# Four held chunks in the output projections, next-stage windows by token tile, and tails as tasks

## The chip, the cores and the metric

The kernel runs on one core of one Trainium2 chip. The metric is device microseconds of one execution, the median of several runs. Engines: TensorE (PE, matmuls; PEld its weight loads), VectorE (DVE), ScalarE (ACT), GpSimd (POOL), and SyncE (SP), whose queue issues the DMAs.

## What is computed

Two transformer-like layers on 256 tokens of width 1024, in float32. The parts that the change touches are the output projections, the residual with its norm behind them, and the first products of the next stage:

```python
# layer 1, end of the mixer
mix = (g_ssd * y_ssd + g_sc * y_sc) @ w_o
x = x + gt1 * rmsnorm(mix, mix_post_g)
h = rmsnorm(x, ffn_pre_g) * (1.0 + sc2) + sh2
u = causal_dwconv(h @ w_up, ffn_conv_w, ffn_conv_b)
u_gate, u_val = jnp.split(u, 2, axis=-1)
f = (jax.nn.silu(u_gate) * u_val) @ w_down
x = x + gt2 * rmsnorm(f, ffn_post_g)
# layer 2
h = rms_norm(x, attn_norm) * (1.0 + scale_a) + shift_a
... = jnp.split(h @ w_in, IN_OFFSETS, axis=-1)          # nc, ns, nw, q, ...
x = x + gate_a * (o @ w_o)                              # no norm on the product
h = rms_norm(x, ffn_norm) * (1.0 + scale_f) + shift_f   # then a second conv FFN, gated by gate_f
```

The modulation rows and columns (gt1, sc2, ...) are products of silu(c) with 1024x1024 blocks of `ada_w` ("ada" below).

## The kernel before

**Weights.** All weights stream from HBM in order of the list `keys`: chunks of 128x2048, each in two halves of 128x1024 (512 KB). `dma_next` loads a half into one of six `raw` tiles. `cast_next` (line 527) splits it: ACT writes `hi` (rounded to fp32r), DVE writes `lo` = raw - hi, into one of five `hlp` slots (HALVES = 5); `caster` does so whenever fewer than `limit[0]` halves are ahead. Each product is three matmuls (hi x hi, lo x hi, hi x lo). A key "ada" isn't cast: `ada_mul` multiplies the half by silu(c) on DVE with a running sum.

**Two product forms.** `chunk_a` (643): weights stationary, 256 token columns moving, 48 matmuls of 128x256 for a chunk of 2x128 features. `b_mm`, `window` and `out_proj`: 128 tokens stationary, 512 weight columns moving, output by token tile t = 0, 1.

**Order.** The instruction streams are written out by a planner (`_Order`): the main code issues PE's work; tasks (generators) issue the work of DVE, ACT and the transposes when their planned time is reached, by rank. Each engine then runs its stream in order.

**Output projections.** `out_proj` (679) runs three times: "wo" (4 chunks, end of the mixer), "dn" (11 chunks, end of the first FFN), "wo2" (4 chunks, end of attention), and "dn2" closes the kernel. All chunks but the last two run for both token tiles; the last two are held in SBUF, all of tile 0's products run first, then tile 1's 24 matmuls of 128x512. `tail_of(t)` follows each.

**Tails.** `tail` (1471) makes the next normalized activations (`h2`, `h3`, `h4`, as hi and lo) of a token tile from the projection in PSUM: square and row sum (`sq`), times the gate row (`mul`), `norm_sum` (POOL raises to -1/2), residual update (`upd`), square of x (`sqx`), `norm_sum`, a diagonal matrix of the norm (`diag`), transposing matmuls x.T @ diag (`turn`), scale and shift (`evA` on ACT, `evV` on DVE), `hi`, `lo`. For "wo2" there is no first norm. The order of these steps, and where weight casts stand among them (`cast:`), is written out by hand in the strings TAILS (line 245); casting is otherwise off (`limit[0] = 0`).

**Filler.** The rows gt2 and gf don't come through `keys`. `adp` (1027) loads their eight halves into `adp` tiles, `adp_add` sums 6 or 7 of them on DVE, and `adp_fill` puts the rest on PE as float32 matmuls of 128x512 inside the tails of "wo" and "wo2" (`fill:`). The other rows are spread over the partitions by `row_sum` (1044) with 8 small matmuls.

**Behind the tails.** In `ffn` (1647) the first two up chunks run in parts ("0a 0b 1a ..."), each on both tiles at once, so they start when both tiles are turned. Behind "dn", `window_split` (1754) runs "nc" for tile 0, lets the tail go on, then for tile 1; "ns" and "nw" follow as windows. `w1` needs the blocks that `nc_task` makes from nc. `wo2_ready` (2402) waits for the tasks `os_task(g, t)`, which make the two halves of the attention output: wo2's chunks 0 and 1 need group 0, chunks 2 and 3 need group 1.

Of the kernel before, what the change touches and what calls it, by code (L numbers as in the profile page):

```python
# [26 lines left out]


ON_PE = ("gt2", "gf")


def _plan():

    plan = []
# [44 lines left out]
    for i in range(22):  # L79
        plan.append((("up", i), 2048, a_pair("w_up", 128 * i, 2816 + 128 * i)))  # L80
# [23 lines left out]
    for i in range(22):  # L104
        plan.append((("up2", i), 2048, a_pair("w_up_2", 128 * i, 2816 + 128 * i)))
# [5 lines left out]
    for nm, (w, s) in {**ADA_ROW, **ADA_COL}.items():  # L111
        for j in range(4):
            plan.append((("ada", nm, j), 2048, b_cols(w, 2 * j, 2, 1024 * s, 1024) if nm in ON_PE else f_rows(w, 1024 * s + 256 * j)))
# [94 lines left out]
def _consts():  # L208
# [33 lines left out]
UPORDER = ("0a 0b 1a 0l 1b 1l", "0a 0b 1a 1b 0l 1l")  # L242
LAST_C = "gt1"
ND = {"gt2": 6, "gf": 7}
TAILS = {
# [170 lines left out]
def _body(ctx: ExitStack, tc: tile.TileContext, wst, pf_d, rows_d, cst_d, xT_d, x_d, w2_d, out_d):  # L416
# [86 lines left out]
    st = {"dma": 0, "cast": 0, "half": 0, "ahead": 0}  # L503
# [23 lines left out]
    def cast_next():  # L527
# [5 lines left out]
        if keys[i][0] == "ada":  # L533
            ada_mul(keys[i][1], 2 * keys[i][2] + hf, r)
        else:
            h = hlp.tile([128, 1024], F32R, name="hi")
            l = hlp.tile([128, 1024], F32R, name="lo")
# [30 lines left out]
    def drop(i, hf):  # L568
        parts.pop((i, hf))
        st["ahead"] -= 1  # L570
        free_at[0] = O.t["pe"]
# [107 lines left out]
    def out_proj(name, nch, x, ready, tail_of, done=lambda c: None):  # L679
# [12 lines left out]
        for c in range(nch - 2):  # L692
            ready(c, 0)
            ready(c, 1)

# [4 lines left out]
            done(c)  # L700
        held = []
        for c in (nch - 2, nch - 1):
# [3 lines left out]
        for t in range(2):  # L706
            for c in (nch - 2, nch - 1):
                ready(c, t)
            for j in range(2):
                for w, c, hf in held:  # L710
# [30 lines left out]
    for w, g in SSD_ORDER:  # L741
        keys += [("scc", g), ("sch", g), ("scb", g)] if w == "sc" else [(w, g, 0), (w, g, 1)]
    so = lambda p: [("so", p, 0), ("so", p, 1)]
# [4 lines left out]
    keys += [("wo", k) for k in range(4)] + [("up", i) for i in range(22)] + [("dn", k) for k in range(11)]  # L748
# [6 lines left out]
    keys += [("up2", i) for i in range(22)] + [("dn2", k) for k in range(11)]  # L755
# [15 lines left out]
    assert sorted(map(str, keys)) == sorted(str(k) for k, _, _ in PLAN if k[0] != "ada0" and k[1] not in ON_PE)  # L771

# [116 lines left out]
    for t in range(8):  # L889
        w = W(t)  # L890

        def half(hf_):
# [7 lines left out]
            st["ahead"] -= 1  # L900

# [16 lines left out]
    limit = [HALVES]  # L918
# [49 lines left out]
    adp_w, adp_sum, adp_ps = {}, {}, {}  # L968

    def adp_load(nm, spared):  # L970

        for k in range(8):
            yield from room(big=1 + spared)
            r = big("adp")
            O.keep("big")
            o, n = CH["ada", nm, k // 2]
            nc.sync.dma_start(r, bass.AP(tensor=wst.tensor, offset=wst.offset + o + 1024 * (k % 2), ap=[[n, 128], [1, 1024]]))
            adp_w[nm].append((r, O.dma(512, O.cur.now)))
            O.cur.now = max(O.cur.now, O.t["dma"] - 1500.0)
# [1476 lines left out]
```

## Time and profile before

| | |
|---|---|
| median of 3 runs | 1071.05 us (1067.59 to 1071.38) |
| the profiled execution | 1072.64 us, of it the span from first to last instruction 1070.7 us |
| PE busy | 1036.2 us (97%), 7183 matmuls |
| DVE busy | 849.8 us (79%) |
| ACT busy | 628.4 us (59%) |
| mean granted clock of PE | 0.982 |

Matmuls are pipelined, so a matmul's cost is the distance from one start to the next, not its duration. PE without a gap isn't PE at its best either: small or needless matmuls count as busy.

### The profile page before, as it was taken

To read this page: it belongs to the slowest core of one execution; us is meant where nothing else is said; L and a number is where in the kernel's file an instruction comes from. 1 tells how busy PE (TensorE), PEld (TensorE's weight loads), DVE (VectorE), ACT (ScalarE), POOL (GpSimd) and SP (SyncE) were. 2 spreads that over 40 slices of the span, in tenths; PEclk is the share of its full clock that TensorE was granted. 3 is DMA by queue.
4 is the path that set the end of the run, shared out by engine and by line. 5 is a ranking of instruction groups with operands and counts; after the bars stand their busy time and mean duration, and the time that the engine had idled before them with its cause. 6 is when DMAs were issued, how large, how long until landed. Compare 5 with 4: busy or idle time off the path is not lost.

```text
span 1070.7 us, 18920 instructions
## 1 busy us (share of the span) xinstructions
PE 1036.2 (97%) x7183; PEld 957.1 (89%) x7183; DVE 849.8 (79%) x1566; ACT 628.4 (59%) x1230; POOL 45.7 (4%) x66
## 2 busy tenths in 40 slices
PE   7999999999999999999999889998999789999998
PEld 7999999899999979999987779877998679999986
DVE  5878978977987768998886888896889687878843
ACT  3457569378654366656554466768675346666531
POOL 2000000000000000000000010221100000000000
PEclk8999999999999999999999989998999989999999
DMA  9855577767868947676686588854256725555551
GB/s 356 310 197 170 176 244 242 238 208 242 284 211 305 328 171 227 223 262 222 225 302 201 188 304 281 291 204 139 77 159 231 281 91 195 180 181 183 188 185 40
DMA packets 66187, 234.03 MB, mean 219 GB/s; under 512 B 7568, under 2 KB 8624, under 8 KB 65584
## 3 DMA queue, kind: packets, MB, share of 16 engines
q1 hardware_dynamic: 66096, 232.82, 64.4%
q8 instruction: 56, 0.92, 0.3%
q14 instruction: 35, 0.29, 0.1%
HBM read 230.67 MB, written 2.13 MB: 217 GB/s over the span
## 4 chain that ended last, share of the span: by engine, by line
PE 52%; DVE 5%; ACT 3%; DMA 2%; issue 1%; POOL 0%; ACTq 0%; DVEq 0%; POOLq 0%
PE ps L410 52%; DVE lo L410 2%; DMA raw<-in_wst_dram 1%; ACT hi L410 1%; DMA adp<-in_wst_dram 1%; ACT S L410 1%; DVE S L410 1%; ACT jk L410 0%; DVE raw L410 0%; DVE jk L410 0%; DVE ropet L410 0%; DVE qo L410 0%; DVE Sm L410 0%; DVE tmp L410 0%; ACT tmp L410 0%
## 5 line engine op out<-in xcount | busy, mean ns | idle before, releaser
L410 DVE TENSOR_TENSOR lo<-raw,hi 128x1024 fp32r<-128x1024 f32 (+3 forms) x326 | 388.2, 1197 | 149.0 <-ACT hi L410 147.9
L410 ACT CAST hi<-raw 128x1024 fp32r<-128x1024 f32 (+3 forms) x326 | 332.9, 1031 | 216.2 <-PE ps L410 170.5
L410 PE MATMUL ps<-hh,hi 128*128 128x256 f32 (+1 forms) x520 | 152.8, 294 | 4.1 <-ACT hh L410 4.1
L410 PE MATMUL ps<-hl,hi 128*128 128x256 f32 (+1 forms) x520 | 148.8, 286 | 0.5 <-DVE hl L410 0.4
L410 PE MATMUL ps<-hh,lo 128*128 128x256 f32 (+1 forms) x520 | 148.6, 286 | 0.0
L410 PEld LDWEIGHTS ps<-hh,hi 128*128 128x128 f32 (+1 forms) x520 | 100.4, 193 | 5.9 <-ACT hh L410 4.5
L410 PE MATMUL ps<-h4h,hi 128*128 128x256 f32 x352 | 100.9, 289 | 2.8 <-ACT h4h L410 2.8
L410 PEld LDWEIGHTS ps<-hl,hi 128*128 128x128 f32 (+1 forms) x520 | 100.4, 193 | 2.3 <-issue 1.2
L410 PE MATMUL ps<-h4h,lo 128*128 128x256 f32 x352 | 100.7, 288 | 0.0
L410 PEld LDWEIGHTS ps<-hh,lo 128*128 128x128 f32 (+1 forms) x520 | 100.4, 193 | 0.1
L410 PE MATMUL ps<-h2h,hi 128*128 128x256 f32 x352 | 98.4, 283 | 0.0
L410 PE MATMUL ps<-h2h,lo 128*128 128x256 f32 x352 | 98.3, 283 | 0.0
L410 PE MATMUL ps<-h2l,hi 128*128 128x256 f32 x352 | 94.7, 283 | 0.0
L410 PE MATMUL ps<-h4l,hi 128*128 128x256 f32 x352 | 94.5, 283 | 0.0
L410 DVE CUSTOM_DVE_ANT_0 raw<-raw,crow 128x1024 f32<-128x1024 f32 x64 | 76.9, 1219 | 0.0
L410 DVE SCALAR_TENSOR_TENSOR fc<-ps,pf,fc 128x254 f32<-128x254 f32 (+1 forms) x176 | 72.4, 474 | 0.0
L410 PEld LDWEIGHTS ps<-h4h,hi 128*128 128x128 f32 x352 | 69.6, 198 | 3.0 <-ACT h4h L410 3.0
L410 PEld LDWEIGHTS ps<-h4h,lo 128*128 128x128 f32 x352 | 69.5, 197 | 0.0
L410 PEld LDWEIGHTS ps<-h2h,hi 128*128 128x128 f32 x352 | 67.6, 192 | 0.8 <-ACT h2h L410 0.8
L410 PEld LDWEIGHTS ps<-h2h,lo 128*128 128x128 f32 x352 | 67.6, 192 | 0.0
L410 PEld LDWEIGHTS ps<-h2l,hi 128*128 128x128 f32 x352 | 65.4, 192 | 0.0
L410 PEld LDWEIGHTS ps<-h4l,hi 128*128 128x128 f32 x352 | 65.4, 192 | 0.0
(394 smaller groups left out, 2363.6 us busy)
## 6 DMA issues: line engine op xcount, KB each, us to landing
raw<-in_wst_dram SPq DMA_DIRECT2D x364, 512.0 KB, 4.9
adp<-in_wst_dram SPq DMA_DIRECT2D x16, 512.0 KB, 7.2
ada0a<-in_wst_dram SPq DMA_DIRECT2D x8, 512.0 KB, 8.0
ada0b<-in_wst_dram SPq DMA_DIRECT2D x8, 512.0 KB, 8.7
E<-scr SPq DMA_DIRECT2D x4, 1024.0 KB, 6.8
raw<-in_wst_dram SPq DMA_DIRECT2D x8, 400.0 KB, 7.5
raw<-in_wst_dram SPq DMA_DIRECT2D x8, 384.0 KB, 7.3
brow<-in_rows_dram SPq DMA_DIRECT2D x4, 512.0 KB, 7.9
```

The source lines that it names most:

```text
L410: return f(*a, **k)
```

## The change

- `out_proj` holds four chunks instead of two ("wo", "dn", "wo2"; "dn2" stays at two): tile 0 runs all held products first, then tile 1 runs 48 matmuls of 128x512. A chunk of the first two held is dropped during tile 1's pass.
- Weight halves beyond five may be cast into pairs of `big` tiles (22 of 128x1024 in all, shared with the activations) while `more[0]` is set and `spared` tiles are left over.
- The tail of each tile is a task (`tail_task`, rank -0.8) whose steps go out as they come due. x is scaled by the norm on ACT and DVE and then transposed (`transpose`, one pass) instead of turned by a diagonal matrix. The strings TAILS, the filler and `adp` are gone. Casting is no longer switched off.
- The next stage begins with two products of 512 columns (`windows`): tile 0 of both, then tile 1 of both. Behind "dn" these are nc and ns. In the FFNs they are the first four up chunks in the 512-column form ("upb"); their outputs are copied by ACT and transposed on PE (`copy_task`, `turn_task`) to the layout that `up_task` wants.
- The rows gt2 and gf come through `keys` like the others (`ada_mul`, then `row_sum` with its 16 small matmuls for two halves), at new places: gt2 behind up 4, sha behind up 11, sca behind up 18, shf behind dn 3 (it was behind ns 0), gf behind up2 10. The activation row is switched from c to c2 behind gt2 (it was behind gt1).
- The tiles of attention that `wo2_ready` released are released by a task.

```diff
+    def up_plan(key, w):
+        for p in range(2):
+            cols = np.concatenate([np.arange(256) + o + 256 * p for o in (0, 2816)])
+            for h in range(2):
+                plan.append(((key + "b", p, h), 2048, b_list(w, 4 * h, 4, cols)))
+        for i in range(4, 22):
+            plan.append(((key, i), 2048, a_pair(w, 128 * i, 2816 + 128 * i)))
...
+SPARED = {"gt1": 6, "gt2": 3, "ga": 3}
+HOLD_GA = 4
+LAST_C = "gt2"
...
+            inner = st["hl"] < HALVES
+            if inner:
+                h, l = hlp.tile([128, 1024], F32R, name="hi"), hlp.tile([128, 1024], F32R, name="lo")
+            else:
+                h, l = big("whi", F32R), big("wlo", F32R)
...
-            yield lambda: st["ahead"] < limit[0] and st["cast"] in raws
+            yield lambda: st["cast"] in raws and (st["hl"] < HALVES or more[0] is not None and O.used["big"] + 2 + more[0] <= CAP["big"])
...
-        for c in range(nch - 2):
+        for c in range(nch - hold):
             ready(c, 0)
             ready(c, 1)
+            if c == nch - hold - 2:
+                more[0] = spared
...
+        more[0] = spared
         held = []
-        for c in (nch - 2, nch - 1):
+        for c in range(nch - hold, nch):
...
         for t in range(2):
+            for w, c, hf in held[:-4]:
+                if not hf:
+                    ready(c, t)
+                if not t:
+                    arrive(w, hf)
+                half(t, w, c, hf)
+                if t:
+                    drop(w.i, hf)
...
-    mix_in("sha", ("up", 8), 2)
-    mix_in("sca", ("up", 20), 4)
+    mix_in("gt2", ("up", 4), 2)
+    mix_in("sha", ("up", 11), 2)
+    mix_in("sca", ("up", 18), 2)
+    mix_in("shf", ("dn", 3), 1)
     mix_in("ga", ("bg", 5), 1)
     mix_in("scf", ("q1", 1), 1)
-    mix_in("shf", ("ns", 0), 2)
+    mix_in("gf", ("up2", 10), 2)
...
+        def tail_task(t, ps):
...
+            r = norm_sum(ss)
+            yield
+            par(lambda: AC.activation(tmp[:, :512], x[:, :512], AF.Identity, scale=r),
+                lambda: VE.tensor_scalar(tmp[:, 512:], x[:, 512:], r, None, op0=OP.mult))
...
+            for f in range(8):
+                transpose(tp[f // 4][:, 128 * (f % 4):128 * (f % 4) + 128], tmp[:, 128 * f:128 * f + 128])
...
+    def windows(names, x, ks, done):
...
+        for t in range(2):
+            O.until(lambda: len(ks) > t and ks[t].done)
+            for n in range(2):
+                ps = bank()
+                for q, (w, hf) in enumerate(held[n]):
+                    arrive(w, hf)
+                    for k in range(2):
+                        kk = 2 * q + k
+                        O.pump()
+                        x.come(kk, 0, (t,))
+                        xh, xl = x.hi(kk, 128 * t, 128), x.lo(kk, 128 * t, 128)
+                        c = hf * 1024 + k * 512
+                        PE.matmul(ps, xh, w.hi(c, 512), start=kk == 0, stop=False)
+                        PE.matmul(ps, xh, w.lo(c, 512), start=False, stop=False)
+                        x.come(kk, 1, (t,))
+                        PE.matmul(ps, xl, w.hi(c, 512), start=False, stop=kk == 7)
...
+        windows([(up + "b", p) for p in range(2)], hh, k_hh, done)
...
-        for i in range(2, 22):
-            ks.append(O.spawn(up_task(i, chunk_a((up, i), hh), w, b, first_is_gate, f)))
+        for i in range(4, 22):
+            ks[i] = O.spawn(up_task(i, chunk_a((up, i), hh), w, b_, first_is_gate, f))
...
-    k_nc = O.spawn(nc_task(window_split("nc", k_h)))
...
+    windows([("nc",), ("ns",)], h, k_h, pw_done)
...
-    adp("gf", 2)
-    out_proj("wo2", 4, osum, wo2_ready, of)
+    out_proj("wo2", 4, osum, wo2_ready, of, hold=HOLD_GA, spared=SPARED["ga"])
```

## Rows read from the trace of the kernel before

**Rows 1.** The page, part 1: busy us, share of span, instructions.

```profile
PE 1036.2 (97%) x7183; PEld 957.1 (89%) x7183; DVE 849.8 (79%) x1566; ACT 628.4 (59%) x1230; POOL 45.7 (4%) x66
```

**Rows 2.** PE's waits: what it waited for, us in total, times, longest.

```profile
PE ps L410 <- DVE Sm L410: 4.4, 3, 3.7
...
PE ps L410 <- DVE ko L410: 4.0, 1, 4.0
```

**Rows 3.** Stretches: length; busy us of PE, PEld, DVE, ACT, POOL; granted clock; DMA.

```profile
398.50:460.00 61.50, 61.50 (x512) 61.50 (x513) 53.39 (x86) 39.01 (x59) 0.00 (x0) 1.00 0.70 224
460.00:526.00 66.00, 66.00 (x550) 65.87 (x548) 58.79 (x103) 39.95 (x66) 0.00 (x0) 1.00 0.73 242
526.00:585.30 59.30, 59.30 (x263) 48.81 (x261) 43.25 (x71) 28.20 (x42) 1.08 (x2) 1.00 0.74 250
...
876.60:882.80 6.20, 6.16 (x29) 6.16 (x30) 4.71 (x6) 3.36 (x4) 0.00 (x0) 0.50 0.39 131
```

**Rows 4.** Timeline of PE, wo's end to up's start: start, us, operation [idle before].

```profile
387.52 0.39 PE L410 MATMUL ps<-hi,mixl 128*128 128x512 f32 x1
...
388.20 0.39 PE L410 MATMUL ps<-hi,mixl 128*128 128x512 f32 x1
389.16 2.05 PE L410 MATMUL ps<-btok,xr 128*128 128x128 f32 x16 [0.58 <-DVE btok L410]
391.05 3.60 PE L410 MATMUL ps<-adp,cb 128*128 128x512 f32 x8
394.70 2.05 PE L410 MATMUL ps<-btok,xr 128*128 128x128 f32 x16
...
398.48 0.39 PE L410 MATMUL ps<-h2h,hi 128*128 128x256 f32 x1
398.70 0.28 PE L410 MATMUL ps<-h2h,lo 128*128 128x256 f32 x1
...
398.94 0.28 PE L410 MATMUL ps<-h2h,lo 128*128 128x256 f32 x1
```

**Rows 5.** Timeline of PE, dn's end to the second tile of nc.

```profile
585.29 2.05 PE L410 MATMUL ps<-btok,xr 128*128 128x128 f32 x16
...
590.20 0.50 PE L410 MATMUL ps<-hi,h3h 128*128 128x512 f32 x1 [2.85 <-ACT h3h L410]
...
599.26 0.50 PE L410 MATMUL ps<-hi,h3h 128*128 128x512 f32 x1 [1.27 <-ACT h3h L410]
```

**Rows 6.** Timeline of PE, wo2's end to up2's start.

```profile
866.44 1.95 PE L410 MATMUL ps<-btok,xr 128*128 128x128 f32 x16
...
876.64 0.58 PE L410 MATMUL ps<-h4h,hi 128*128 128x256 f32 x1 [2.79 <-ACT h4h L410]
```

**Rows 7.** Timeline of ACT, dn's tail of tile 0: last square, first hi half.

```profile
579.99 0.60 ACT L410 ACTIVATE jk<-ps 128x512 f32<-128x512 f32 x1 [2.03 <-PE ps L410]
...
589.50 0.64 ACT L410 CAST h3h<-jk 128x512 fp32r<-128x512 f32 x1
```

**Rows 8.** Timeline of PE: a row sum's half, and four one-pass transposes.

```profile
347.39 1.05 PE L410 MATMUL ps<-cst,mod_gt 128*128 128x128 f32 x8
348.20 0.36 PE L410 MATMUL ps<-yTh,hi 128*128 128x256 f32 x1
...
834.72 0.60 PE L410 MATMUL ps<-cst,S 128*128 128x128 f32 x4
835.07 0.70 PE L410 MATMUL ps<-hi,osh 128*128 128x512 f32 x2
```

**Rows 9.** Timeline of DVE, the end of attention.

```profile
850.24 1.28 DVE L410 SCALAR_TENSOR_TENSOR adp<-adp,cact 128x1024 f32<-128x1024 f32 x1 [1.57 <-DMA adp<-in_wst_dram]
851.44 0.35 DVE L410 TENSOR_SCALAR Sm<-Sm,sumsm 128x256 f32<-128x256 f32 x1
```

**Rows 10.** DVE groups by shape: busy us, mean ns, idle before them.

```profile
L410 DVE TENSOR_TENSOR lo<-raw,hi 128x1024 fp32r<-128x1024 f32 x300 | 364.3, 1221 | 146.6 <-ACT hi L410 145.6
L410 DVE CUSTOM_DVE_ANT_0 raw<-raw,crow 128x1024 f32<-128x1024 f32 x64 | 76.9, 1219 | 0.0
```

More of the change, by code (lines that the diff above doesn't have):

```diff
@@ L502, in _body @@
     raws, parts, landed, cast_at = {}, {}, {}, {}
-    st = {"dma": 0, "cast": 0, "half": 0, "ahead": 0}
+    st = {"dma": 0, "cast": 0, "half": 0, "ahead": 0, "hl": 0}
+    home, more = {}, [None]
     units = []
@@ L1034, in ada_task @@
             O.cur.now += 1000
-            yield from row_sum(nm, [], m)
+            yield from row_sum(nm, m)
         else:
@@ L1042, in ada_task, with row_sum @@
             yield
[L1044 removed]
+    def row_sum(nm, a):
         yield ada_row[nm]
@@ L1430, in _body @@
     so_k(1, 1)
-    adp("gt2", 5)
     for p in (2, 3):
@@ new lines, in tail @@
+    def tail(gname, post, name, a, sh):
+        hh = HL(name)
+        ks = []
+        def tail_task(t, ps):
+            yield ada_k[gname]
+            yield from room(big=1, a2=1)
+            G, x = MOD[gname], xr[t]
+            tmp, jk = big("tmp"), a2("jk")
+            half = [slice(0, 512), slice(512, 1024)]
+            if post:
+                ss = sm.tile([128, 2], F32, name="ss")
+                for j in range(2):
+                    par(lambda: AC.activation(jk, ps[j], AF.Square, accum_out=ss[:, j:j + 1]),
+                        lambda: VE.tensor_mul(tmp[:, half[1 - j]], ps[1 - j], G[:, half[1 - j]]))
+                yield
+                free(*ps)
+                r = norm_sum(ss)
+                yield
+            ss = sm.tile([128, 2], F32, name="ss2")
+            for j in range(2):
@@ L1527, in mod @@
-            def mod(t, q, ks, act):
-                for k in ks or range(4):
+                    VE.tensor_mul(tmp[:, half[j]], ps[j], G[:, half[j]])
+                    free(ps[j])
+                    VE.tensor_add(x[:, half[j]], x[:, half[j]], tmp[:, half[j]])
+            n = O.cur.now
+            for j in range(2):
+                O.cur.now = n - 600.0 * (1 - j)
+                AC.activation(jk, x[:, half[j]], AF.Square, accum_out=ss[:, j:j + 1])
+            yield
+            r = norm_sum(ss)
@@ L1602, in gen @@
-            O.cur = pieces
-            for _ in fl:
-                pass
-            for k in (hold, pieces):
-                for tag, n in k.held.items():
-                    O.used[tag] -= n
-            O.cur = None
-            limit[0] = HALVES
-        parts = gen()
-        def tail_of(t, ps):
-            limit[0] = 0
-            pss[t] = ps
-            for j in range(2):
-                ends["pe", t, j] = O.t["pe"] - 2500.0 * (1 - j)
-            next(parts, None)
-        hh.rest = lambda: next(parts, None)
@@ L1621, in tail @@
-        return hh, [], tail_of
+            par(lambda: ev(True), lambda: ev(False))
+            free(*tp)
+            for q in range(2):
+                yield from hh.room(4 * q)
+                hh.part(4 * q, 0)
+            for x_ in range(2):
+                for q in range(2):
+                    o = [hh.part(4 * q, p).rearrange("p (f t) -> p f t", f=4)[:, :, 128 * t:128 * t + 128] for p in range(2)]
+                    i = y[q].rearrange("p (f t) -> p f t", f=4)
+                    if x_:
+                        VE.tensor_sub(o[1], i, o[0].bitcast(F32))
+                    else:
+                        AC.copy(o[0], i)
+                    hh.at[q, t, x_] = O.cur.now + 200.0
@@ new lines, in tail_of @@
+        def tail_of(t, ps):
+            ks.append(O.spawn(tail_task(t, ps), -0.8))
+        return hh, ks, tail_of
+    def windows(names, x, ks, done):
+        held = [[], []]
+        for n, nm in enumerate(names):
+            for ch in range(2):
+                step((*nm, ch), lambda w, hf: held[n].append((w, hf)), hold=True)
+        for t in range(2):
[14 more added lines that the diff above has]
+                        PE.matmul(ps, xl, w.hi(c, 512), start=False, stop=kk == 7)
+                    if t:
+                        drop(w.i, hf)
+                    elif n and q == 3:
+                        more[0] = None
+                done(n, t, ps)
@@ new lines, in ffn, with copy_task, turn_task @@
+        ks, ux, k_tr = {}, {}, []
+        def copy_task(n, t, ps):
+            yield from room(a2=1)
+            ux[n, t] = a2("ux")
+            O.keep("a2")
+            AC.copy(ux[n, t], ps)
+            free(ps)
+            yield
+        def turn_task(n, k):
+            yield k
+            O.adopt("a2", 2)
+            pss = []
+            for i in range(2):
+                b = yield from tbank()
+                pss.append(b)
+            for i in range(2):
+                for j in range(2):
+                    for t in range(2):
+                        transpose(ab(pss[i], j)[:, 128 * t:128 * t + 128], ux[n, t][:, 256 * j + 128 * i:256 * j + 128 * i + 128])
+            O.rel("a2", 2)
+            yield
+            for i in range(2):
+                ks[2 * n + i] = O.spawn(up_task(2 * n + i, pss[i], w, b_, first_is_gate, f))
@@ L1720, in _body @@
     k_tab = O.spawn(tab_task())
-    h, k_h, of = tail("gt2", True, "h3", "sca", "sha", None)
+    h, k_h, of = tail("gt2", True, "h3", "sca", "sha")
     phase_is(1)
-    ffn("up", "dn", h2, k_h2, "fw", "fb", True, of)
+    ffn("up", "dn", h2, k_h2, "fw", "fb", True, of, spared=SPARED["gt2"])
     phase_is(2)
```

305 lines of the change are left out of this document (72 added, 233 removed), and 3 rows, old and new, of the table TAILS.

## The prediction, made before the changed kernel was run

> **What bounds the kernel now.** The page comes first: PE is busy for 97% of the span, DVE for 79% [rows 1]. So the time can fall in three ways only: less PE work, shorter PE work, or fewer PE gaps. PE's waits come next, to see how little there is in gaps: the span of 1070.7 us less PE's busy time is 34.5 us, and two of the longest single waits are one for DVE's `Sm` at the end of attention (3.7 us) and one for `ko` behind nw (4.0 us) [rows 2]. The third view is PE's timeline at the three places where a tail stands between an output projection and the next stage. Here the reader should look at what PE does, not whether it is busy:
> - Behind wo, the last product starts at 388.20 and up starts at 398.48. With 0.23 us for that product, 10.05 us go by with no product of the model in them: two turns of 16 passes (1.9 us each, 389.16 to 391.05), float32 filler (391.05 to 394.70, and the rest up to 398.48), and a gap of under a microsecond [rows 4].
> - Behind dn, 585.29 to 599.26 is 13.97 us, of which nc's first tile is 24 products; the gaps are 2.85 and 1.27 us [rows 5].
> [...]
>
> **Prices.** A product of 512 columns takes (388.20 - 387.52)/3 = 0.227 us, one of 256 columns (398.94 - 398.70)/2 = 0.12 us [rows 4]. Eight one-pass transposes cost 2 x 0.35 = 0.7 us, from four in 834.72 to 835.07; one half of a row sum costs 348.20 - 347.39 = 0.81 us [rows 8]. A cast's `lo` and an `ada_mul` cost DVE 1.22 us each [rows 10].
>
> **The tails.** What the change gives each tail as cover: tile 1's pass over four chunks is 48 x 0.227 = 10.9 us for tile 0's tail, and tile 0's pass over the two windows is another 10.9 us for tile 1's. What a tail takes: dn's tile 0, in a hand-written order with a few casts between, goes from its last square at 579.99 to the end of its first `hi` half at 590.14, 10.15 us [rows 7]. The new chain is alike: the scaling of x takes the place of the diagonal, the transposes are 1.2 us shorter than a turn, but the steps now stand in DVE's stream among casts that go out when they are due. Each such cast can push a step back by 1.22 us [rows 10]; there are six DVE steps in the chain and about four casts in the pass, so from 0 to 5 us, and I take 2.5. That makes 12.5 us against 10.9. I take a wait of 2 us for tile 0 and 1 us for tile 1, since tile 0's wait also delays the pass behind it. The clock: of the two waits of about 2.8 us in the old tails one was followed by the low clock (3.1 us lost) and one was not [rows 3, 5, 6], so half, 1.5 us. Bounds for wait and clock together are 0 and 10 us for each place.
> - Behind wo: 10.05 becomes 1.4 (16 transposes) + 4.5, so -4.1.
> - Behind dn: 13.97 - 24 x 0.227 = 8.5 becomes 5.9, so -2.6.
> - Behind wo2: 10.2 + 3.1 = 13.3; there is no first norm here, the chain is about 2 us shorter, so 1.4 + 2.5 and -9.4.
>
> **Work on PE that comes and goes.** The filler and the two-pass turns are already in these sums. Four up chunks as `chunk_a` are 192 x 0.12 = 23.0 us, as windows 96 x 0.227 = 21.8 us: -1.25 in each FFN, -2.5. The new layout needs 16 transposes in each FFN, 2 x 1.4 = +2.8, among other products; ACT's four copies hide in its 41% of idle time [rows 1]; if they didn't, PE's transposes behind them would wait, not the up chunks. Rows gt2 and gf now need `row_sum`: 2 x 2 x 0.81 = +3.2.
>
> [...]
>
> **The end of attention.** DVE's stream stood on an `adp` load: `adp_add` waited 1.57 us for a DMA and ran 1.28 us at 850.24, with the scaling of `Sm` behind it in the queue [rows 9], and PE waited 3.7 us for that [rows 2]. This goes, up to -3.7, and some clock with it. Against it: with two held chunks, wo2's chunks 0 and 1 gave PE 48 products for both tiles before group 1 of the attention output was needed; now only tile 0's 24 stand there, 5.4 us less cover in a chain that waits for latencies. Between -5 and +5; I take -2, the removed wait being the one that a row shows.
>
> **nc to w1.** PE waited 4.0 us behind nw [rows 2]. The eight `ada_mul` of shf, 9.8 us of DVE [rows 10], leave the stretch from nc on; but nc's second tile now ends before ns's second tile, not before all of ns, so that `nc_task` has 5.4 us less time. From -7 (gap gone, clock kept) to +5; I take 0.
>
> **DVE in the first FFN.** From 398.5 to 585.3 DVE is busy 53.4 + 58.8 + 43.3 = 155.4 of 186.8 us, 83%, and 89% in its fullest stretch [rows 3]. gt2 and shf add 16 `ada_mul`, 19.5 us; sca's eight move forward into the up chunks. 175 us is 94% of that time. Five cast halves and a few PSUM banks of waiting `up_task`s cushion it. From 0 to +16 (below); I take +2. Moved with it: the row c2 is loaded behind gt2 on SP's queue, only two halves ahead of sha's first multiply, so ACT's silu of it can stand for a few us with casts behind it; five halves ahead, 14 us of PE work, cover that. The DMAs are the same bytes; the `adp` loads leave the stretch before wo, shf's go to dn.
>
> **Sum**, on the profiled execution: -4.1 - 2.6 - 9.4 - 2.5 + 2.8 + 3.2 - 2 + 0 + 2 = -12.6, 1072.6 to 1060.0 us. That execution is 1.6 us above the median of the runs shown, so I say 1059.
>
> **Rivals.**
> - *The cover is whole.* The tails fit into 10.9 us and PE never waits: the three places cost 1.4 each, 11.5 us less than above; with the gap behind nw gone too, 1041 to 1049. For it: an undisturbed chain is 10.15 us. Against: DVE must cast up to sixteen halves around each boundary.
> - *The tails wait behind casts.* `hi` comes 16 us after the projection, wait 7 us and clock 3 us at each place: 11.4 against 10.05, 8.5 and 13.3. The places together then give +2.3, the rest of the sum +3.5; 1066 to 1077. It decides when a chain loses more than four casts' time. [...]
> - *DVE becomes the bound in the first FFN (slower).* If DVE can't be kept above the 89% that its fullest stretch shows [rows 3], waits for ACT's `hi` being part of its stream (146 us in all [rows 10]), then the 18 up chunks run at DVE's pace. From 460 to 526 DVE does 58.8 us in the time of 66/5.76 = 11.5 chunks, 5.1 us each, of it at most 0.85 for sha's eight multiplies; 20 multiplies on 18 chunks make 1.36 more, so 5.6 to 6.5 us of DVE against 48 x 0.12 = 5.76 us of PE. With 5.9 at 89%, a chunk takes 6.6 us: 18 x 0.87 = +16 us in place of the +2, and two or three low clocks, +3 to 6. It gives 1077 to 1080, from 1074 with a little less. It decides when a chunk wants more of DVE than 89% of 5.76 us and the cushion is used up; the cushion speaks against it.
> - *No effect as said* would be if the planner found no room for the halves beyond five, so that tile 0 waits for casts before its tail begins; the price is that of the second rival.
>
> **How the numbers follow.** Chances: forecast (1050 to 1066) 0.48; whole cover 0.16; tails behind casts 0.16; DVE bound 0.20. A measurement of this kernel can tell about 0.5%, so faster means below 1065.7 and slower above 1076.4. Faster: the first two, 0.64 less the forecast's upper edge, 0.62. Slower: most of the last and the upper end of the third, 0.21. Between: 0.17. The range leaves out a tenth on each side: 1044 to 1080.
>
> **What would show it.** In the profile after: between wo's last product and the next product only 8 transposes and a gap of 1 to 3 us, the same again a pass later, no `adp` rows, the wait for `Sm` smaller; DVE above 90% from the first up chunk to dn 6 with PE still without gaps. Wrong would be: gaps of over 5 us at a tail, PE waits for `lo` or for a bank inside up or dn, or more waiting at the end of attention than the 4.4 us now.

## The result, and the profile after

The changed kernel takes 1101.89 us (median; 1098.96 to 1106.18), the kernel before 1071.22 us in the same comparison. The ratio is 1.029 with a 95% interval of 1.026 to 1.032: the change makes the kernel about 3% slower. The forecast was 1059 us and its range ended at 1080.

The page of after, part 1 (busy time, share of the span, instructions), to be read beside [rows 1]:

```profile
PE 1044.6 (95%) x6987; PEld 956.1 (87%) x6987; DVE 854.2 (77%) x1583; ACT 634.7 (57%) x1244; POOL 49.4 (4%) x66
```

PE has 196 fewer instructions and is still busy for 8 us longer: more of its work ran at a low granted clock (0.50), and the mean granted clock of the span went from 0.982 to 0.962. The span, now 1104.3 us, less PE's busy time grew from 34.5 to 59.7 us. What PE waited for in the whole span (us in total, times, longest), beside [rows 2]:

```profile
PE ps L409 <- ACT tmp L409: 8.8, 2, 4.4
PE ps L409 <- ACT h3h L409: 5.5, 1, 5.5
PE ps L409 <- ACT h2h L409: 5.3, 1, 5.3
PE ps L409 <- ACT fc L409: 4.3, 1, 4.3
...
PE ps L409 <- DVE Sm L409: 3.5, 2, 2.8
PE ps L409 <- DVE wlo L409: 2.9, 3, 1.7
```

The first three are the tails behind wo and dn: PE waits first for the scaled x (`tmp`), which it has to transpose, and then for the first `hi`. The `ko` wait of before is down to 0.9 us, and `Sm` has only come down from 4.4 to 3.5.

The spans of the two profiled executions are 33.6 us apart (that of after is the slowest of its four, 1106.18 us). To see where they lie, the span is cut at starts of products on PE's timeline; each stage runs from one such start to the next, good to 0.2 us. All numbers are us, of the profiled execution of each kernel; the head, up to wo's first product, ran 3.7 us longer in that of after, at a mean granted clock of 0.97 against 0.98, and is left out: most of the experiments with the same head don't have it (366.6 us in e1 as in before; 370.3 in after, 370.1 in e5). The runs in the other columns are told of below.

| stage on PE | before | after | e1 | e2 | e5 | e9 | e7 |
|---|---|---|---|---|---|---|---|
| wo, last product to first of up | 10.3 | 12.1 | 0.2 | 2.0 | 12.1 | 2.0 | 10.3 |
| up | 126.7 | 139.6 | 147.1 | 139.2 | 132.7 | 130.4 | 129.9 |
| dn | 59.8 | 68.5 | 70.6 | 70.1 | 61.9 | 61.7 | 66.3 |
| dn, last product to first of nc | 5.3 | 12.1 | 0.2 | 2.0 | 12.1 | 1.9 | 5.3 |
| nc to the first of wo2 | 237.6 | 237.7 | 245.9 | 233.0 | 235.6 | 234.8 | 236.9 |
| wo2 | 38.4 | 41.0 | 41.1 | 40.8 | 42.3 | 41.1 | 33.4 |
| wo2, last product to first of up2 | 10.4 | 2.0 | 0.2 | 0.2 | 2.0 | 0.2 | 11.9 |
| up2 | 129.4 | 134.0 | 138.3 | 131.3 | 132.3 | 131.2 | 131.1 |

So 21.7 us are lost in up and dn, 1.8 and 6.8 us at the two tails that were to become shorter, 0.8 in wo itself, and 8.4 us are won at the third, of which up2 and wo2 give back 4.6 and 2.6. Of up's 12.9 us, 3.7 are PE's own work in the new layout (e9, below); most of the rest are a wait of 4.31 us, some 2.4 us of low clock behind it (0.50 from 530.5 to 536), and some 2.5 us of low clock behind the tail (0.50 from 404.8 to 409.7).

PE's timeline behind wo in after (start, us, operation, idle time before it and what ended it), beside [rows 4]:

```profile
392.73 0.39 PE L409 MATMUL ps<-whi,mixl 128*128 128x512 f32 x1
397.53 1.97 PE L409 MATMUL ps<-cst,tmp 128*128 128x128 f32 x8 [4.41 <-ACT tmp L409]
404.79 0.79 PE L409 MATMUL ps<-whi,h2h 128*128 128x512 f32 x1 [5.29 <-ACT h2h L409]
```

PE stands for 4.41 and 5.29 us, and its next product takes 0.79 us in place of 0.39. What the tail of token tile 0 was doing all that time stands in DVE's timeline of the same stretch:

```profile
382.28 1.29 DVE L409 TENSOR_TENSOR tmp<-ps,brow 128x512 f32<-128x512 f32 x2 [2.43 <-PE ps L409]
384.73 1.23 DVE L409 TENSOR_TENSOR lo<-raw,hi 128x1024 fp32r<-128x1024 f32 x1 [1.16 <-ACT hi L409]
385.87 0.21 DVE L409 TENSOR_SCALAR r<-ss 128x1 f32<-128x1 f32 x1
386.09 2.58 DVE L409 TENSOR_TENSOR lo<-raw,hi 128x1024 fp32r<-128x1024 f32 x2
388.59 1.41 DVE L409 SCALAR_TENSOR_TENSOR xr<-tmp,r,xr 128x512 f32<-128x512 f32 x2
391.87 1.23 DVE L409 TENSOR_TENSOR lo<-raw,hi 128x1024 fp32r<-128x1024 f32 x1 [1.87 <-ACT hi L409]
393.01 0.21 DVE L409 TENSOR_SCALAR r<-ss 128x1 f32<-128x1 f32 x1
393.13 1.22 DVE L409 TENSOR_TENSOR lo<-raw,hi 128x1024 fp32r<-128x1024 f32 x1
394.27 1.22 DVE L409 TENSOR_TENSOR wlo<-raw,whi 128x1024 fp32r<-128x1024 f32 x1
395.40 1.28 DVE L409 TENSOR_TENSOR tmp<-ps,brow 128x512 f32<-128x512 f32 x2
396.60 0.47 DVE L409 TENSOR_SCALAR tmp<-xr,r 128x512 f32<-128x512 f32 x1
...
398.44 1.23 DVE L409 TENSOR_TENSOR wlo<-raw,whi 128x1024 fp32r<-128x1024 f32 x1 [1.25 <-ACT whi L409]
399.58 1.41 DVE L409 SCALAR_TENSOR_TENSOR xr<-tmp,r,xr 128x512 f32<-128x512 f32 x2
400.91 1.36 DVE L409 TENSOR_SCALAR tmp<-ps,mod_sc,mod_sh 128x128 f32<-128x128 f32 x4
```

The steps of tile 0 are `tmp` at 382.28, `r`, `xr` at 388.59, `r` at 393.01, `tmp<-xr,r` at 396.60 and the modulation at 400.91. Among them stand seven `lo` and `wlo` of weight halves, 7 x 1.22 = 8.5 us, and from 395.40 on also tile 1's steps. By the marks of [rows 7], from ACT's last square of tile 0 to the end of its first `hi` half, the chain takes 21.7 us, where the old order needed 10.15; on ACT's timeline:

```profile
383.07 0.60 ACT L409 ACTIVATE jk<-ps 128x512 f32<-128x512 f32 x1 [2.78 <-DVE tmp L409]
...
404.10 0.63 ACT L409 CAST h2h<-jk 128x512 fp32r<-128x512 f32 x1
```

The stretches of after, beside [rows 3] (length; busy us of PE, PEld, DVE, ACT, POOL; granted clock; DMA share, GB/s):

```profile
381.90:404.80 22.90, 13.20 (x59) 10.55 (x57) 16.24 (x25) 15.19 (x29) 4.11 (x4) 0.81 0.56 191
...
412.00:423.00 11.00, 11.00 (x50) 9.09 (x50) 0.69 (x1) 1.99 (x4) 0.00 (x0) 1.00 0.01 1
...
480.00:526.00 46.00, 46.00 (x386) 46.00 (x385) 45.02 (x73) 24.95 (x38) 0.00 (x0) 1.00 0.90 316
...
544.40:613.00 68.60, 63.98 (x267) 50.90 (x265) 58.51 (x102) 35.98 (x56) 1.49 (x1) 0.95 0.80 276
```

The reader should see that DVE's work is lumped. While PE runs tile 1 through the windows (412 to 423), every weight slot is held for both tiles; nothing is cast and nothing is loaded (1 GB/s), and DVE does 0.69 of 11 us. By 526 it has not caught up: it is busy for 45.02 of the 46 us just ahead, and there PE at last stands. Three waits of up and dn on PE's timeline:

```profile
530.53 0.55 PE L409 MATMUL ps<-h2h,hi 128*128 128x256 f32 x1 [4.31 <-ACT fc L409]
...
548.39 0.47 PE L409 MATMUL ps<-hi,fh 128*128 128x512 f32 x1 [1.43 <-DVE fc L409]
...
593.22 0.50 PE L409 MATMUL ps<-wlo,fh 128*128 128x512 f32 x1 [1.74 <-DVE wlo L409]
```

For the 5.5 us behind the first one the granted clock is 0.50: the products of 256 columns start 0.213 us apart in them and 0.120 us behind them, so 26 products lose 2.4 us. In that gap DVE stands too, on its own timeline:

```profile
527.26 1.22 DVE L409 TENSOR_TENSOR lo<-raw,hi 128x1024 fp32r<-128x1024 f32 x1 [1.65 <-ACT hi L409]
```

That `hi` had waited 1.83 us for a product of PE, and the steps of `fc` that PE waits for stand behind the `lo` in DVE's stream, from 528.40 on. So a full DVE comes first, and at the end the order of its stream adds to the gap.

### The profile page after: what moved, and what is told of

Its sections match the earlier page's. It is cut to its first block, busy times and chain, and to the rows that moved or that the text cites. A ratio compares the mean times of both kernels' runs of the same rounds, so it can differ in the third digit from the quotient of the medians.

```text
span 1104.3 us, 18536 instructions
## 1 busy us (share of the span) xinstructions
PE 1044.6 (95%) x6987; PEld 956.1 (87%) x6987; DVE 854.2 (77%) x1583; ACT 634.7 (57%) x1244; POOL 49.4 (4%) x66
## 4 chain that ended last, share of the span: by engine, by line
PE 41%; DVE 12%; ACT 5%; issue 3%; DMA 2%; POOL 0%; DVEq 0%; ACTq 0%; POOLq 0%
PE ps L409 41%; DVE lo L409 3%; DVE fc L409 3%; DMA raw<-in_wst_dram 2%; ACT hi L409 2%; DVE wlo L409 1%; DVE raw L409 1%; ACT jk L409 1%; ACT S L409 1%; ACT whi L409 1%; DVE fl L409 1%; DVE S L409 0%; DVE tmp L409 0%; ACT junk L409 0%; DVE xr L409 0%
## 5 line engine op out<-in xcount | busy, mean ns | idle before, releaser
L409 DVE TENSOR_TENSOR lo<-raw,hi 128x1024 fp32r<-128x1024 f32 (+4 forms) x306 | 362.8, 1194 | 154.8 <-ACT hi L409 153.1
L409 ACT CAST hi<-raw 128x1024 fp32r<-128x1024 f32 (+4 forms) x306 | 311.6, 1027 | 186.9 <-PE ps L409 138.6
L409 DVE CUSTOM_DVE_ANT_0 raw<-raw,crow 128x1024 f32<-128x1024 f32 x80 | 96.1, 1217 | 5.3 <-ACT crow L409 5.1
L409 PE MATMUL ps<-h2h,hi 128*128 128x256 f32 x280 | 80.7, 288 | 4.3 <-ACT fc L409 4.3
L409 PE MATMUL ps<-h2h,lo 128*128 128x256 f32 x280 | 80.3, 287 | 0.0
L409 PE MATMUL ps<-h4h,lo 128*128 128x256 f32 x280 | 79.4, 284 | 0.7 <-DVE lo L409 0.7
L409 PE MATMUL ps<-h4h,hi 128*128 128x256 f32 x280 | 79.4, 284 | 0.0
L409 ACT ACTIVATE fc<-ps,pf 128x256 f32<-128x256 f32 x88 | 45.0, 561 | 32.1 <-PE ps L409 13.3
L409 PEld LDWEIGHTS ps<-h4h,lo 128*128 128x128 f32 x280 | 53.7, 192 | 1.0 <-DVE lo L409 0.9
L409 PE MATMUL ps<-hi,fh 128*128 128x512 f32 x164 | 52.7, 392 | 1.8 <-DVE fc L409 1.8
```

The lines of the kernel that those rows point to most:

```text
L409: return f(*a, **k)
```

## The experiments

Theory A: VectorE is what binds. It pays for the sixteen added multiplies in up and dn, and for the eight weight halves that the windows want at once around each tail. Theory B: the transfers and weight slots bind up and dn. Theory C: only the order matters, casts standing ahead of the tail's steps in DVE's stream. The expectations of e1 to e4 have letters of their own; from e5 on they use these.

**e1: no cast while a tail is open** (`tails_open` counts the tails under way).

```
-  yield lambda: st["cast"] in raws and (...)
+  yield lambda: not tails_open[0] and st["cast"] in raws and (...)
```

> The changed kernel with no weight cast while a tail is open; nothing else is changed. Theory A (the steps of a tail queue behind casts on DVE and ACT, which makes a tail 22 us long instead of 10): the first hi half of tile 0 comes 10 to 12 us after its projection at each of the three places, PE has no gap ahead of tile 0's transposes, but now PE waits for the weights of the windows, some 3 to 6 us at each place; in all 1090 to 1100 us against 1102. Theory B (the new chain is long by itself, by its order and by scaling x ahead of the transposes): hi still comes 15 us or more after the projection, and the time rises above 1105 us.

Measured: 1100.31 us, ratio 1.029 (1.026 to 1.032). With no cast among its steps the tail fits whole under tile 1's pass: up's first product follows wo's last after 0.2 us, and so at all three places. By the marks of [rows 7] the chain behind wo takes 8.7 us (379.35 to 388.03). But nothing is won, and the total just misses the 1090 to 1100 us that was expected. PE's waits between 388 and 440 us of e1 (total, times, longest):

```profile
PE ps L409 <- ACT tmp L409: 4.0, 1, 4.0
PE ps L409 <- ACT hi L409: 3.1, 1, 3.1
```

PE now stands for tile 1's transposes and for the weights that weren't cast, up is 7.5 us longer than in after, and the stage behind dn 8.2 us. So the casts among its steps explain how long the tail is (theory C is right in that), and to put them all off wins nothing: what was moved out of the way has to be done a moment later.

**e2: the `lo` of halves cast while a tail is open left out**, `hi` standing in for it; ACT's half of the cast, the loads and the slots stay.

```
+  if tails_open[0]: l = h
+  else:
       VE.tensor_sub(l[:, :b - a], r, h[:, :b - a].bitcast(F32))
```

> The changed kernel with DVE's share of the casts left out while a tail is open: the lo parts of those weight halves aren't computed, the hi parts stand in for them (the output is not the reference's). Theory A: DVE's queue is what the tails wait in; the two waits at each place fall from 4.4 and 5.3 us to under 2 us, tile 0's hi comes 13 us or less after its projection, 1078 to 1090 us. Theory B: the waits stay within 1 us of what they are, 1098 us or more.

Measured: 1073.77 us, ratio 1.0035 (1.0022 to 1.0048), less than theory A's 1078 to 1090. With 21 subtractions (25.6 us of DVE) left out, 28.1 us go, and they go where the tails are: 10.1 us behind wo, 10.1 behind dn, 1.7 behind wo2, 4.7 between nc and wo2, 2.7 in up2. Up and dn together are not shorter (209.3 us against 208.2). By the marks of [rows 7] the chain behind wo takes 12.5 us (379.36 to 391.81), so of after's 21.7 us DVE's casts are 9.2, and ACT's the 3.8 between e2 and e1. Beside e1 this says that DVE's work around the tails is what is paid. That no order of the same work would do isn't shown: e1 put off ACT's casts too, and in after DVE is busy for 16.24 of the 22.9 us from 381.9 to 404.8, so an order in which casts only fill its idle time is left untested.

**e3: the row c2 loaded early**, into a tile of its own, so that ACT's silu of it doesn't hold up sha's first multiply.

```
+  c2row.append(big("crow2"))
+  row_load(c2row[0], "c2")
...
-  crow_load("c2")
```

> The changed kernel with the row c2 loaded early into a tile of its own, so that only ScalarE's silu stands between the last gt2 multiply and the first sha multiply. Theory C (DVE's 5.1 us of idleness behind the row's load in a stretch in which DVE is full is what makes PE wait 4.3 us at the end of up, with a low clock behind it): the wait and the low clock go, 1093 to 1097 us. Rival (DVE is too full anyway and the wait moves to another place in up or dn): 1099 to 1104 us.

Measured: 1099.98 us, ratio 1.028 (1.025 to 1.031), the rival's outcome. In after this is the third longest of DVE's waits between 400 and 612 us, on DVE's timeline:

```profile
472.34 1.23 DVE L409 CUSTOM_DVE_ANT_0 raw<-raw,crow 128x1024 f32<-128x1024 f32 x1 [5.10 <-ACT crow L409]
```

Without it up takes 134.4 us, 5.2 less, and dn 74.7, 6.2 more. The stall was real; DVE still has the same work, so the wait moves on.

**e4: two chunks held in all three projections, not four.**

```
-  out_proj("wo", 4, mix, wo_ready, of, spared=...)
+  out_proj("wo", 4, mix, wo_ready, of, hold=2, spared=...)
... (dn and wo2 likewise)
```

> The changed kernel with two held chunks instead of four in all three projections; casts into the large tiles, the windows and the tails as tasks stay. Theory A (casts in the tails are the harm, the longer pass is a help): tile 0's cover is 5.4 us shorter, so its wait at each place is 3 to 5 us longer, 1108 to 1118 us. Rival (holding four chunks is the harm, by the casts and tiles it ties up): 1085 to 1095 us.

Measured: 1096.99 us, ratio 1.025 (1.023 to 1.028): neither outcome. Fewer halves held brings up to 134.4 us and dn to 72.4, together 1.4 us less, and the places behind wo and dn to 11.3 each; behind wo2 the place is back at 12.2, with wo2 2.6 us shorter; nc to wo2 is 5.8 us shorter. So four held chunks are worth 10.2 us at wo2's tail, where the chain is short, and cost more than that elsewhere: with two held the changed kernel is 4.9 us faster.

**e5: gt2's and shf's multiplies shortened** to 64 of 1024 columns.

```
+  n_ = 64 if nm in ("gt2", "shf") else 1024
-  VE.tensor_tensor_reduce(out=w, in0=w, in1=crow, ...)
+  VE.tensor_tensor_reduce(out=w[:, :n_], in0=w[:, :n_], in1=crow[:, :n_], ...)
```

> The changed kernel, but each multiply of gt2's and shf's sixteen halves covers 64 of its 1024 columns (the vectors are then wrong: a part of the sums is left out); every transfer, slot and order stays. It takes 16 x about 1.1 = 18 us of work off DVE between the first up product and dn 6, and no byte off the DMA queues. Theory A (VectorE is the bound of the first FFN; its added multiplies are paid one for one): 1082 to 1090 us, with the stretch from the first h2 product to the last dn product some 12 to 18 us shorter than the 208 us of the changed kernel. Theory B (the transfers, 0.99 of the DMA engines in 560 to 580, and the weight slots bound it): 1097 to 1103 us, the stretch within 3 us of 208. Theory C (the whole loss lies in the tails' order on DVE and is carried on): 1097 to 1103 us as well, but with DVE below 90% busy in that stretch.

Measured: 1086.60 us, ratio 1.016 (1.010 to 1.021). Up and dn together fall from 208.2 to 194.5 us. dn's stretch in e5:

```profile
537.20:599.00 61.80, 60.87 (x266) 49.12 (x265) 48.00 (x93) 33.85 (x50) 1.49 (x1) 1.00 0.87 306
```

Every wait of over 0.5 us inside up and dn is gone, and the DMA engines are busier than in after (0.87 against 0.80 in the same stage), moving the same bytes in less time (61.8 us at 306 GB/s against 68.6 at 276). That is theory A; theory B falls for the transfers. A shorter multiply also frees its loading tile earlier, by an estimate of 1.1 us (960 of the 1024 columns that take 1.22), so the slots aren't told apart from DVE's time.

**e6: shf and sca put back** where they stood before.

```
+  mix_in("sca", ("up", 20), 4)
+  mix_in("shf", ("ns", 0), 2)
-  mix_in("sca", ("up", 18), 2)
-  mix_in("shf", ("dn", 3), 1)
```

> The changed kernel with shf's and sca's halves put back where they stood before (shf beside the windows of attention, sca over the end of up and dn); gt2 stays in up. Eight multiplies of 1.22 us (9.8 us) and 4 MB of transfers leave the first FFN for the start of attention. Theory A (VectorE is full in the first FFN): dn comes back from 68.5 us to 60 to 63 us, the attention grows by 0 to 4 us, 1091 to 1098 us. Theory C (the tails carry the loss): 1099 to 1104 us, since what dn saves is waited for at its tail.

Measured: 1092.92 us, ratio 1.022 (1.017 to 1.027), as theory A has it in total, but not in place. Up gains 7.6 us (sca has left most of it) and dn only 0.8: shf's multiplies are gone from dn, sca's are there instead, and three waits of 1.4 to 2.1 us for DVE's and ACT's `fc` stand at its start.

**e7: one part alone, in the kernel before**: gt2 and gf over the weight stream, no filler; tails, slots and first up chunks as before. The switch of the row c and sha's place move with gt2.

```
-ON_PE = ("gt2", "gf")
+ON_PE = ()
...
+  mix_in("gt2", ("up", 4), 2)
+  mix_in("sha", ("up", 11), 2)
+  mix_in("gf", ("up2", 10), 2)
-  adp("gt2", 5)
-  adp("gf", 2)
```

> The kernel before with one part of the change alone: gt2 and gf come in halves over the weight stream, as in the changed kernel, their PE filler (20 transposes' worth of 512-column products per vector) and their separate loads are gone; tails, weight slots and first up chunks stay as they were. If the added multiplies of gt2 in up are paid (theory A): the first FFN grows by 6 to 10 us, the end of attention loses its waits for the adp sums (4 to 9 us): 1066 to 1076 us. If the vectors are not the trouble (theory C, the casts between the tails' steps): 1060 to 1067 us. If the tails of before need the filler to cover their chain (the clock falls without it): 1077 to 1085 us.

Measured: 1075.27 us, ratio 1.005 (1.003 to 1.007). It tells three things. With gt2's eight multiplies (9.8 us of DVE) up and dn are 9.7 us longer. That the two are so near is chance: of up's 3.2 us, 1.6 are PE's row sum, and the rest goes with a mean granted clock of 0.99 over up (1.00 in before); dn's 6.5 are mostly one wait of 2.9 us for `fc` at its start and the low clock behind it (0.82 from 526 to 536, 0.95 over dn). The adp sums of gf cost 5.1 us at the end of attention (wo2 38.4 to 33.4). And the filler of before cost PE no time. PE's timeline behind wo in e7:

```profile
394.17 2.05 PE L410 MATMUL ps<-btok,xr 128*128 128x128 f32 x16 [3.48 <-DVE btok L410]
397.95 0.39 PE L410 MATMUL ps<-h2h,hi 128*128 128x256 f32 x1 [1.73 <-ACT h2h L410]
```

Where the filler was there are now gaps of 3.48 and 1.73 us, and the place is as long as before, 10.3 us: the chain of the tail set its length. Over up, behind it, the mean granted clock is 0.99, where before, with its filler, has 1.00.

**e8: gf alone** of those two, in the kernel before.

```
-ON_PE = ("gt2", "gf")
+ON_PE = ("gt2",)
+  mix_in("gf", ("up2", 10), 2)
-  adp("gf", 2)
```

> The kernel before with gf alone taken from the filler into the weight stream of the second FFN. Theory A and C alike: no adp sum delays the softmax at the end of attention (Sm 4.4, ko 4.0 of waits), and the second FFN has VectorE to spare (8 x 1.22 us): 1061 to 1067 us. Rival, the filler of this tail is what keeps PE's clock up between wo2 and up2: 1070 to 1076 us.

Measured: 1066.86 us, ratio 0.9974 (0.9954 to 0.9995). Wo2 takes 33.4 us as in e7, and up2, which has DVE to spare, grows by 0.6. It is the one version that computes everything and is faster than both kernels, by a quarter of a per cent.

**e9: e2 and e5 together**, to see whether the two costs are one.

```
(the edits of e2 and of e5)
```

> Two edits of earlier runs together: the lo halves cast while a tail is open are left out (28 us less when alone), and gt2's and shf's multiplies cover 64 of 1024 columns (15 us less when alone); parts of the computation are left out, so the output isn't the reference's. If the two costs are separate terms, one in the tails and one in the first FFN, they add: 1101.9 - 28.1 - 15.3 = 1058.5, 1054 to 1063 us. If both take away the same wait for VectorE, the second brings little: 1068 to 1075 us.

Measured: 1059.85 us, ratio 0.992 (0.990 to 0.995), with both pieces of work missing. The sum of the two single effects gave 1058.5: they are two separate bills. PE behind wo in e9:

```profile
389.26 0.39 PE L409 MATMUL ps<-whi,mixl 128*128 128x512 f32 x1
391.21 0.50 PE L409 MATMUL ps<-whi,h2h 128*128 128x512 f32 x1 [1.56 <-ACT h2h L409]
```

and the stretch of up in e9:

```profile
391.20:521.60 130.40, 130.39 (x999) 125.82 (x1000) 109.15 (x204) 80.51 (x132) 1.08 (x2) 1.00 0.77 261
```

Up has no gap of note and full clock and takes 130.4 us: that is its PE work in the new layout, 3.7 us more than before.

**e10: the `lo` of every third half of up and dn on POOL**, outside the tails.

```
+  if not tails_open[0] and phase[0] == 1 and u % 3 == 0:
+      nc.gpsimd.tensor_sub(l[:, :b - a], r, h[:, :b - a].bitcast(F32))
+  else:
       VE.tensor_sub(l[:, :b - a], r, h[:, :b - a].bitcast(F32))
```

> The changed kernel, but outside the tails the lo of every third weight half of the first FFN is subtracted on POOL, which is idle there; nothing is left out. Some 20 subtractions of 1.22 us leave VectorE (24 us of 208). From the multiply of 128x256 on POOL in the kernel before (923 ns) an estimate for 128x1024 is 3.7 us. Theory A (VectorE's work is the bound there): 1080 to 1090 us, the first FFN 12 to 18 us shorter. Rival (POOL's longer subtraction comes late for PE, or slows VectorE beside it): 1098 to 1112 us.

Measured: 1096.72 us, ratio 1.027 (1.022 to 1.031), between the two expectations. Up and dn are 5.8 us shorter, not 12 to 18. POOL took 19 subtractions (18 are in the group below), faster than estimated; but the ones that stayed on DVE became longer. POOL's group in e10 (count, busy us, mean ns):

```profile
L546 POOL TENSOR_TENSOR lo<-raw,hi 128x1024 fp32r<-128x1024 f32 x18 | 47.2, 2624 | 138.4 <-ACT hi L409 130.6 <-DVE fl L409 7.9
```

and DVE's groups from 400 to 612 us of e10, to be read beside 1221 ns in [rows 10]:

```profile
L409 DVE TENSOR_TENSOR lo<-raw,hi 128x1024 fp32r<-128x1024 f32 x41 | 58.2, 1428 | 16.4 <-ACT hi L409 16.2
L409 DVE CUSTOM_DVE_ANT_0 raw<-raw,crow 128x1024 f32<-128x1024 f32 x32 | 40.2, 1283 | 3.5 <-ACT crow L409 3.5
L409 DVE TENSOR_TENSOR fl<-fc,fh 128x256 fp32r<-128x256 f32 x22 | 21.1, 972 | 0.0
```

These three groups alone have grown by 8.5 + 2.0 + 12.2 = 22.7 us (41 x 0.21, 32 x 0.06 and 22 x 0.55; `fl` took 417 ns in after), and 19 x 1.22 = 23.2 us had been taken off DVE.

**e11: the same, and every second half inside the tails on POOL too.**

```
+  if u % 2 == 0 if tails_open[0] else phase[0] == 1 and u % 3 == 0:
```

> As the run before it, and while a tail is open the lo of every second half goes to POOL too, four of some eight per tail. If VectorE's subtractions between the tail's steps are what lengthens it: 4 x 1.22 = 5 us per tail less, 6 tails in part hidden, so 5 to 15 us below the run before it: 1068 to 1083 us. Rival: the tail's two powers run on POOL and now wait up to 3.7 us each behind a subtraction: 0 to 10 us above the run before it.

Measured: 1094.59 us, ratio 1.023 (1.019 to 1.027), 2.1 us below e10: neither outcome. The place behind wo shrinks from 12.1 to 0.6 us, but wo itself grows by 4.2 and up by 8.2.

**e12: e11 with the positions of e6.**

```
(the edits of e11 and of e6)
```

> As the run before it, with shf's and sca's halves put back where they stood before the change (9 us less when done alone). If POOL has already taken VectorE below its bound in the first FFN: within 3 us of the run before it. If VectorE is still the bound there: 4 to 9 us below it.

Measured: 1095.22 us, ratio 1.024 (1.020 to 1.028), the same as e11. By the expectation this would say that VectorE no longer binds up and dn. The trace doesn't bear that out: the place behind dn falls from 11.7 to 2.7 us, and nc to w1 grows from 40.8 to 50.7. The wait has moved again, and the run settles nothing by itself.

## Why the prediction was wrong

**What bounds the kernel.** PE at 97% was read rightly for the kernel before. What failed are two terms of the sum, and both are DVE's. The first is "from 0 to 5 us, and I take 2.5", what casts do to the chain of a tail: DVE's casts made it 9.2 us longer (21.7 us in after, 12.5 in e2). The second is the +2 for DVE in the first FFN: with the added multiplies cut short up and dn are 13.7 us shorter (e5).

The prediction did ask how many casts fall into a pass, but DVE's time was costed by shares of long stretches, 83% and 89%, and never summed between two dates of PE around a boundary. There the new form leaves it no room. The windows need all eight halves of two chunk pairs before the pass of tile 0 is over: 8 x 1.22 = 9.8 us. The two tiles' own steps, from the rows of DVE above, are 1.29 + 1.41 + 0.47 + 1.36 and two `r`, 5.0 us for a tile, and two `lo` of h2 more for each. 9.8 + 2 x 5.0 = 19.8 us, without those, stand against the 21.8 us that both passes last, in a chain that also waits for other engines; and while PE is in the windows the held slots keep DVE from working ahead (0.69 of 11 us).

**Prices.** They held, but for the transposes: eight take 0.8 to 0.9 us in e9, not 0.7. Products of 512 columns still start 0.227 us apart in dn, of 0.39 us each, and DVE's groups by shape in after are, beside [rows 10] (busy us, mean ns):

```profile
L409 DVE TENSOR_TENSOR lo<-raw,hi 128x1024 fp32r<-128x1024 f32 x280 | 339.0, 1220 | 149.9 <-ACT hi L409 148.5
L409 DVE CUSTOM_DVE_ANT_0 raw<-raw,crow 128x1024 f32<-128x1024 f32 x80 | 96.1, 1217 | 5.3 <-ACT crow L409 5.1 <-DMA raw<-in_wst_dram 0.2
...
L409 DVE TENSOR_TENSOR fl<-fc,fh 128x256 fp32r<-128x256 f32 x44 | 18.1, 417 | 0.0
```

**The tails.** The chain was put at 12.5 us with 2.5 us of DVE's casts in it. Without them it takes 12.5 us, not 10 (six of ACT's casts stand in it in e2, two in the old chain), and then the gap behind wo is 1.56 us (e2 and e9 alike have a place of 2.0 us), where the forecast for a chain of 12.5 said 2. So what a chain of that length costs was sized well, and the casts were not: seven of DVE's stood there, not two, and the chain lasted 21.7 us. Part of it is POOL's: its two powers take 1.56 and 1.46 us beside DVE's casts, not 0.55 (last section). The two places came to 12.1 us each where the forecast left 5.9. The filler that was to be saved behind wo was no saving: without it the old place is as long (e7). Behind wo2 there is no first norm and the weights are cast in time; 8.4 us were won there, where 9.4 with the clock had been forecast, but up2 gave back 4.6. Of the 13.3 us that the forecast gave the old place, 10.2 are those of [rows 6]; the other 3.1, half of 6.2 us, no run shows: in the stretch at 0.50 of [rows 3] products of 256 columns start 0.213 us apart (877.02 to 882.57) and behind it 0.120 (883.02 to 885.90), so its 29 products lose 2.7 us.

**Work on PE.** -2.5 + 2.8 + 3.2 = +3.5 us was forecast for both FFNs. Summed from start to start on PE's timeline of e9, the windows take 22.4 and 22.2 us (21.8 forecast), the 16 transposes 1.8 and the row sum 1.6 us in each FFN: -1.5 + 3.5 + 3.2 = +5.2. So the term was too small by 1.7 us. The windows' gain is 1.5 us, where 2.5 was forecast. The eight transposes of a tile's x, 0.8 us, stand in up, dn and up2 as well; the forecast has them in the tails.

**The end of attention.** "I take -2." The removed `adp` sums are worth 5.1 us (e7, e8), more than the 3.7 us wait that a row showed. The lost cover and the new waits cost more: wo2 went up to 41.0, 2.6 above before and 7.6 above e7; with two held chunks it is 38.5 (e4). The bounds held, the sign of the middle did not.

**nc to w1.** 0 was forecast, and -0.4 measured (42.4 to 42.0).

**DVE in the first FFN.** +2 was taken, on the word of a cushion: "Five cast halves and a few PSUM banks". The sixteen multiplies cost 13.7 us there (e5), by waits and by the low clock behind them (a mean of 0.96 over up and 0.95 over dn in after, 0.98 and 1.00 in e5). So the cushion that was to cover all but 2 us was small; that nothing is cast from 412 to 423 fits this. The claim that five halves ahead cover ACT's silu of c2 failed too, 5.1 us of DVE's time, though to mend it moved the wait only (e3).

**The rivals.** Two of them came true at once: "the tails wait behind casts" and "DVE becomes the bound in the first FFN". Each was given a time as if the other did not happen, and the range was built from single rivals. Taken together, from the prediction's own terms, they give 2.3 + 3.5 - 2 + 16 + 4.5 = +24 us, 1097 us from the profiled 1072.6, near the 1102 measured. The total is nearer than its parts: DVE was not held to 89% (45.02 of 46 us is 98%), up lost its time in one stop and the clock behind it and not by 0.87 us a chunk, and the place behind wo2 came to 2.0 us and not 11.4. That the two costs add is what e9 shows. That rivals resting on one engine's spare time tend to come together is the step that the chances missed.

That e9 lands at 1059.85, on the forecast number, is partly chance: its tails are shorter than forecast and its PE work longer. It does show that those two costs of DVE, both of them work that the kernel needs, are the difference between 0.8% faster and 2.9% slower.

**What would show it.** The list of signs did its work: gaps of over 5 us at two tails and PE waits for `wlo` and for banks inside up and dn were named as the signs of a wrong forecast, and all of them are in the profile.

## What to carry to other kernels

An engine that is off the critical path needs its budget made out for the few us around each stage boundary, not as a share of a stage: count what it must do between two dates of the bounding engine, and ask what keeps it from working ahead (here, slots held for a second pass). When a wait moves and the total stays, as in e1, e3 and e12, take the work itself away, and then take two suspects away together to see whether they add. Rivals that draw on the same spare time should be priced as a sum.

## What the runs showed of the hardware

In the stretch of e10 below, operations of POOL and DVE that began while the other engine was in one took longer than most of their kind. POOL began a subtraction at 462.70 while DVE was in a multiply, and DVE's next `lo` began at 463.79 (DVE's timeline):

```profile
462.64 1.21 DVE L409 CUSTOM_DVE_ANT_0 raw<-raw,crow 128x1024 f32<-128x1024 f32 x1
...
463.79 3.39 DVE L409 TENSOR_TENSOR lo<-raw,hi 128x1024 fp32r<-128x1024 f32 x1
```

and POOL's:

```profile
462.70 3.39 POOL L546 TENSOR_TENSOR lo<-raw,hi 128x1024 fp32r<-128x1024 f32 x1 [8.95 <-ACT hi L409]
```

POOL's operation took 3.39 us, where four others between 439 and 500 us took 2.41 to 2.50: some 0.9 us more, and DVE's multiply ended 1.15 us after POOL's start. It ended at 466.09, and DVE's `lo` 1.09 us after that, at 467.18, which is nearly the mean of 1.22 us in after. Read so, the two take turns; the trace gives their times and not what makes them do it. Not all of DVE's operations grew: the multiply-adds `fc<-ps,pf,fc` kept their 0.47 us, and `fc<-fc,fc` its 0.41 us (413 ns, 416 in after).

The same is to be seen in after itself. POOL's two powers in tile 0's tail behind wo:

```profile
386.16 1.56 POOL L409 TENSOR_TENSOR r<-r,nhalf 128x1 f32<-128x1 f32 x1 [69.47 <-DVE r L409]
393.30 1.46 POOL L409 TENSOR_TENSOR r<-r,nhalf 128x1 f32<-128x1 f32 x1 [5.58 <-DVE r L409]
```

Each begins within 0.2 us behind the start of a `lo` of DVE (386.09 and 393.13). Tile 1's two, at 397.28 and 402.47 where DVE does nothing, take 0.54 us each. In before, e1 and e2, where DVE casts nothing beside them, the two take 0.55 us each.

The length of a gap doesn't tell by itself what the clock does after it. In before the 2.79 us behind wo2 [rows 6] are followed by 6.2 us at a granted clock of 0.50 [rows 3], and the 2.85 us behind dn [rows 5] leave it at 1.00 to 630. In e9 PE stands behind wo for 1.56 us, and the clock is 1.00 over all of up; in e2 PE stands there for the same 1.56 us, and the mean over up is 0.96, but PE has 4.3 us of idle time inside up as well. In after it is 0.50 for 5.5 us behind the 4.31 us gap at 526, and 0.50 from 594.1 to 600.9 behind the 1.74 us gap at 593, in a stretch with one more gap of 1.01 us. In e7 the gaps of 3.48 and 1.73 us behind wo are followed by a mean of 0.99 over up.
